# Rstd divided out of the residual around four feed-forwards, their seven products chained through one bank, and own tiles for weight sums

## The chip, the cores and the metric

The kernel runs on one core of a Trainium2 chip. The metric is the device time of one execution in microseconds. TensorE multiplies, VectorE and ScalarE read the results out of the PSUM banks and do the elementwise work, GpSimd takes some of it, and SyncE issues the loads of the weights.

## The reference

The inputs are 512 tokens of width 1024 in float32. A first block (attention of two kinds, then a feed-forward with a short convolution) is followed by a second block of two layers. Each layer of the second block has two feed-forwards with half weight and a mixer between them:

```python
def swiglu(x, w_gate, w_up, w_down):
    return (jax.nn.silu(x @ w_gate) * (x @ w_up)) @ w_down
...
    for l in range(DEPTH_2):
        h = x + 0.5 * swiglu(rms_norm_2(x, ffn1_norm[l]), ffn1_gate[l], ffn1_up[l], ffn1_down[l])
        u = rms_norm_2(h, mix_norm[l])
        ...
        h = h + jnp.concatenate([y_da, y_sc, y_lru], axis=-1) @ w_out[l]
        x = h + 0.5 * swiglu(rms_norm_2(h, ffn2_norm[l]), ffn2_gate[l], ffn2_up[l], ffn2_down[l])
    return rms_norm_2(x, final_norm)
```

The gate and up matrices are 1024 x 2816, the down matrix 2816 x 1024. The change concerns these four feed-forwards.

## The kernel before

The running output `xT` lies in SBUF with features on partitions: eight tiles `xT[:, k, :]` of 128 features by 512 tokens. Every float32 operand of a product is split into a rounded part (`hi`, a ScalarE copy, L155) and a remainder (`lo`, a VectorE subtraction, L159), and a product is three passes: hi x hi, hi x lo, lo x hi. Three pairs of buffers hold split weights (`halves`), five hold weights as loaded (`weights2`).

The hidden 2816 features are worked off in eleven pairs of 128-feature tiles (`pair(t)` in `swiglu_pair`). For each pair, gate and up together are a 2 x 2 block product with half the tokens by half the features, done in seven products in place of eight (`seven`, L225). A product is 24 matmuls of 256 columns (L239 to L241). Weights of the products are sums of blocks: `seven_weights` makes them on VectorE (L209) in a buffer `sums` from the pool `big`, which has two buffers. Pairs alternate between two sets of three banks, (mm, mm, mm) and (sc, sc, o); inside a pair the seven products go to the banks a, d, b, a, b, d, b, and those that return to a bank are accumulated on what stands there:

```python
        for i, (bank, (xh, xl)) in enumerate(zip((a, d, b, a, b, d, b), x)):
```

The seven activations come from `Seven.add` and `Seven.put` (L355 to L388). As each output tile k becomes final, it is multiplied by the gain into `xg`, two tiles of the pool `big`; its squares are added to `acc`. After k = 3 the activations 1 and 5 are split; after k = 7 the other five (L380 to L387).

The normalisation is not applied to the activations: R, the reciprocal root of the mean square, is a row per token that multiplies the results. `Norm.step` first sums `acc` over partitions on TensorE (L261), then VectorE adds eps (L252) and GpSimd takes the power (L247); at its second call TensorE spreads the result over all partitions (L269) and ScalarE copies it to `norm.R` (L287). In a pair, R multiplies the gate before the silu on VectorE and after it on GpSimd (both L1227, a helper's line), so that the product with the up half carries it once more.

`ffn` (L1202) runs `pair` eleven times. From the fourth pair on, each is followed by half a down group: 48 matmuls of 512 columns into two banks `ptr` (L181 to L183), which take two finished pairs to four of the eight output tiles, and `update` adds -0.5 times the bank to `xT` (L1374). The last six tiles come in one group at the end; there `update` also calls `nxt.add`. In the last feed-forward this group is done with tokens on partitions (`final`).

The second block's tables (bias, lambda factors, polynomial for a softplus, block-diagonal weights) are made where the block begins, between the first block's last down product and the first pair (L1303 to L1362).

Each engine runs its instructions in the order of its own queue. That order is made by a scheduler when the kernel is built: it follows the order of the program and takes an instruction early where it expects its inputs and buffers to be there. A tile pool's buffer is given out again after the last read of what was in it.

## Time and profile before

| | us |
|---|---|
| median of three runs | 2653.69 (2651.96 to 2656.13) |
| the profiled execution | 2657.64 |
| its span, first to last instruction | 2655.8 |

The profile shows for each engine when it was busy and what ended its idle time; L12 is line 12 of the kernel. Busy time of TensorE includes matmuls that are stretched or overlap. PEclk is the granted share of TensorE's full clock. "Waits" puts a wait for several things down to the last of them. Below, the head of a feed-forward is the time from its first product to its first down product.

### The profile page before, as it was taken

To read this page: it belongs to the slowest core of one execution; us is meant where nothing else is said; L and a number is where in the kernel's file an instruction comes from. 1 tells how busy PE (TensorE), PEld (TensorE's weight loads), DVE (VectorE), ACT (ScalarE), POOL (GpSimd) and SP (SyncE) were. 2 spreads that over 40 slices of the span, in tenths; PEclk is the share of its full clock that TensorE was granted. 3 is DMA by queue.
4 is the path that set the end of the run, shared out by engine and by line. 5 is a ranking of instruction groups with operands and counts; after the bars stand their busy time and mean duration, and the time that the engine had idled before them with its cause. 6 is when DMAs were issued, how large, how long until landed. Compare 5 with 4: busy or idle time off the path is not lost.

```text
span 2655.8 us, 38263 instructions
## 1 busy us (share of the span) xinstructions
PE 2525.5 (95%) x15256; PEld 2189.1 (82%) x15256; DVE 1963.0 (74%) x2887; ACT 1189.1 (45%) x1758; POOL 435.9 (16%) x334
## 2 busy tenths in 40 slices
PE   5999989999979999999989999899999999899998
PEld 4886668888868999887789999799988877789998
DVE  8788786555589787666688887798886566798774
ACT  4357644333344434356344433544344455444433
POOL 3256220000011111023111111011110222011110
PEclk9999999999989999999989999899999999899999
DMA  8332253333233332421223333233333312233331
GB/s 255 115 107 64 72 159 96 93 91 95 87 113 96 98 108 93 139 72 56 80 72 104 106 101 96 73 103 104 104 96 104 119 56 72 63 103 98 104 108 68
DMA packets 318774, 261.62 MB, mean 99 GB/s; under 512 B 10203, under 2 KB 310619, under 8 KB 318596
## 3 DMA queue, kind: packets, MB, share of 16 engines
q1 hardware_dynamic: 313184, 250.98, 30.8%
q10 hardware_dynamic: 5412, 8.20, 0.9%
q8 instruction: 120, 1.97, 0.3%
q14 instruction: 58, 0.48, 0.1%
HBM read 257.03 MB, written 4.74 MB: 99 GB/s over the span
## 4 chain that ended last, share of the span: by engine, by line
PE 47%; DVE 13%; DMA 4%; issue 3%; ACT 2%; POOL 1%; DVEq 0%; POOLq 0%; ACTq 0%; SPq 0%
PE ptr L181 5%; PE ptr L182 4%; PE ptr L183 4%; PE pmm L239 4%; PE pmm L240 4%; PE pmm L241 4%; DVE lo L159 4%; DMA raw<-in_ffn_up 4%; PE pmm L181 3%; PE pmm L183 3%; PE pmm L182 3%; DVE uf L1227 2%; DVE g L1227 2%; PE psc L240 1%; PE psc L239 1%
## 5 line engine op out<-in xcount | busy, mean ns | idle before, releaser
L155 ACT ACTIVATE hi<-raw 128x1024 fp32r<-128x1024 f32 (+3 forms) x434 | 448.5, 1034 | 649.5 <-issue 165.4
L159 DVE TENSOR_TENSOR lo<-raw,hi 128x1024 fp32r<-128x1024 f32 (+2 forms) x402 | 490.0, 1220 | 239.9 <-ACT hi L155 239.4
L239 PE MATMUL pmm<-gh,hi 128*128 128x256 f32 x1344 | 383.1, 285 | 12.9 <-DVE u L1227 9.3
L241 PE MATMUL pmm<-gh,lo 128*128 128x256 f32 x1344 | 380.9, 284 | 2.3 <-DVE lo L159 2.3
L240 PE MATMUL pmm<-gl,hi 128*128 128x256 f32 x1344 | 380.8, 283 | 0.0
L1227 POOL TENSOR_TENSOR g<-g,R 128x512 f32<-128x512 f32 x88 | 167.9, 1908 | 1067.6 <-ACT g L1240 1067.6
L181 PE MATMUL ptr<-uh,hi 128*128 128x512 f32 x832 | 331.0, 398 | 8.8 <-DVE xT L1374 5.0
L183 PE MATMUL ptr<-uh,lo 128*128 128x512 f32 x832 | 329.0, 395 | 0.0
L182 PE MATMUL ptr<-ul,hi 128*128 128x512 f32 x832 | 328.8, 395 | 0.0
L239 PEld LDWEIGHTS pmm<-gh,hi 128*128 128x128 f32 x1344 | 258.8, 193 | 16.3 <-ACT hi L155 14.3
L241 PEld LDWEIGHTS pmm<-gh,lo 128*128 128x128 f32 x1344 | 259.5, 193 | 3.1 <-DVE lo L159 3.0
L240 PEld LDWEIGHTS pmm<-gl,hi 128*128 128x128 f32 x1344 | 256.9, 191 | 0.9
L155 ACT ACTIVATE hi<-sums 128x1024 fp32r<-128x1024 f32 x132 | 139.7, 1059 | 212.6 <-PE ptr L182 119.7
L181 PEld LDWEIGHTS ptr<-uh,hi 128*128 128x128 f32 x832 | 156.1, 188 | 59.0 <-issue 18.6
L183 PEld LDWEIGHTS ptr<-uh,lo 128*128 128x128 f32 x832 | 156.2, 188 | 37.8
L182 PEld LDWEIGHTS ptr<-ul,hi 128*128 128x128 f32 x832 | 156.3, 188 | 34.0
L241 PE MATMUL psc<-gh,lo 128*128 128x256 f32 x640 | 180.0, 281 | 1.0 <-DVE lo L159 1.0
L239 PE MATMUL psc<-gh,hi 128*128 128x256 f32 x640 | 179.3, 280 | 0.0
L240 PE MATMUL psc<-gl,hi 128*128 128x256 f32 x640 | 179.2, 280 | 0.0
L159 DVE TENSOR_TENSOR lo<-sums,hi 128x1024 fp32r<-128x1024 f32 x132 | 160.2, 1214 | 9.1 <-ACT hi L155 8.9
L181 PE MATMUL pmm<-hh,hi 128*128 128x512 f32 x400 | 159.5, 400 | 3.4 <-ACT hh L745 2.3
L183 PE MATMUL pmm<-hh,lo 128*128 128x512 f32 x400 | 158.8, 398 | 2.8 <-DVE lo L159 2.8
(404 smaller groups left out, 5863.7 us busy)
## 6 DMA issues: line engine op xcount, KB each, us to landing
raw<-in_ffn_gate SPq DMA_DIRECT2D x88, 512.0 KB, 3.6
raw<-in_ffn_up SPq DMA_DIRECT2D x88, 512.0 KB, 3.6
raw<-in_ffn_down SPq DMA_DIRECT2D x64, 512.0 KB, 3.4
raw<-in_w_in SPq DMA_DIRECT2D x60, 512.0 KB, 3.9
raw<-in_w_up SPq DMA_DIRECT2D x44, 512.0 KB, 3.8
wa<-in_w_ada SPq DMA_DIRECT2D x80, 256.0 KB, 2.9
raw<-in_ffn_down SPq DMA_DIRECT2D x32, 384.0 KB, 3.4
raw<-in_w_down SPq DMA_DIRECT2D x16, 512.0 KB, 3.3
```

Source lines behind the costliest of these rows:

```text
L155: nc.scalar.activation(out=hi, in_=v, func=AF.Copy)
L159: e.tensor_tensor(out=lo, in0=v, in1=hi.bitcast(F32), op=ALU.subtract)
L181: mm(ps, hi[:, k, c], xh, start=(k == 0), stop=False)
L182: mm(ps, hi[:, k, c], xl, start=False, stop=False)
L183: mm(ps, lo[:, k, c], xh, start=False, stop=(k == kt - 1))
L239: mm(o, hi[:, k, c], xh[:, k, :], start=first, stop=False, skip_group_check=True)
L240: mm(o, hi[:, k, c], xl[:, k, :], start=False, stop=False, skip_group_check=True)
L241: mm(o, lo[:, k, c], xh[:, k, :], start=False, stop=(j == 1 and k == 3), skip_group_check=True)
L1227: tt = lambda e, out, a, b, op: e.tensor_tensor(out=out, in0=a, in1=b, op=op)
```

## The change

- `seven` sends the seven products to the banks b, d, b, a, b, d, b: four of them are now accumulated in b one after the other, and what each partial sum is needed for is copied out (`s`, `s5`, `w`, on ScalarE) or added to a copy (`g1`, `v2`, `g2`) before the next product goes in. The last sum in b is multiplied with the gate straight from the bank.
- R multiplies only the gate before the silu, now on VectorE for both halves; the products with R on GpSimd go. In their place `over_rstd` divides `xT` by R before the first down group is added (`norm.inverse()`: reciprocal, eight small matmuls for the rows, a copy, and one multiplication for each tile), and multiplies it by R again after the last. In the final stage the factors ride in a copy's scale and in the scalar of the update.
- `norm.step()` stands after the third product and `norm.now()` after the fourth, both with high priority for the scheduler.
- Even pairs take the weight sums from a pool of their own of two tiles (`sums`), odd pairs from `big` as before.
- The second block's tables are made in the first block's feed-forward, at its fifth pair, with a tile of `big` as scratch; its pool `u4` has eight buffers in place of nine.
- Pools of the feed-forwards and the mixer are opened with `reuse_waits="tile"`, so that a new tile waits for the old tiles in its place and not for the whole pool.

```diff
-    def seven_weights(self, srcs):
+    def seven_weights(self, srcs, odd):
 
         a11, a21, a22 = (self.load(src, 4, 256) for src in srcs[:3])
         add = lambda o, p, q: self.nc.vector.tensor_tensor(out=o, in0=p, in1=q, op=ALU.add)
-        sums = self.big("sums").rearrange("p (s k c) -> p s k c", s=2, k=4)
-        s1, s2 = sums[:, 0], sums[:, 1]
+
+        if odd:
+            sums = self.big("sums").rearrange("p (s k c) -> p s k c", s=2, k=4)
+            s1, s2 = sums[:, 0], sums[:, 1]
+        else:
+            s1, s2 = (self.quad(self.ap, n, F32).rearrange("p (k c) -> p k c", k=4) for n in ("s1", "s2"))
         yield self.piece(a11)
         add(s1, a21, a22)
         yield self.piece(s1)
...
-        for i, (bank, (xh, xl)) in enumerate(zip((a, d, b, a, b, d, b), x)):
+        ws = self.seven_weights(srcs, odd)
+        for i, (bank, (xh, xl)) in enumerate(zip((b, d, b, a, b, d, b), x)):
             hi, lo = next(ws)
             for j in range(2):
                 o, c = bank[:, j * HALF:j * HALF + HALF], slice(j * P, j * P + P)
                 for k in range(4):
 
-                    first = i < 3 and j == 0 and k == 0
+                    first = i in (0, 1, 3) and j == 0 and k == 0
                     mm(o, hi[:, k, c], xh[:, k, :], start=first, stop=False, skip_group_check=True)
                     mm(o, hi[:, k, c], xl[:, k, :], start=False, stop=False, skip_group_check=True)
...
+    def inverse(self):
+
+        if self.inv is None:
+            net = self.net
+            self.inv = net.up.tile([P, T], F32, tag="inv", name="inv", bufs=1)
+            ic = net.tiny(NB, "ic")
+            net.nc.vector.reciprocal(out=ic, in_=self.rc)
+            net.nc.scalar.activation(out=self.inv, in_=net.rows(ic), func=AF.Copy)
+        return self.inv
 
     def after(self, tiles):
...
 
-    with tc.tile_pool(name="u4", bufs=U_BUFS) as net.up, tc.tile_pool(name="ada2", bufs=2) as adap:
+    bp = net.ctx.enter_context(tc.tile_pool(name="b2", bufs=1))
+    tables = []
+    with tc.tile_pool(name="u4", bufs=U_BUFS - 1, reuse_waits="tile") as net.up, \
+            tc.tile_pool(name="ada2", bufs=2, reuse_waits="tile") as adap:
         mods = ada(range(20, 24), adap)
 
         def pair(t):
+            if t == 8:
+                tables.extend(second_block_tables(net, bp))
             for _ in range(2):
...
 
-    def down(g0, n, chunks, last):
+    def down(i, g0, n, chunks):
         for ci in chunks:
             src = wd[g0 * P:(g0 + n) * P, ci * 256:(ci + 1) * 256]
             for j, ps in net.lin_fm(src, n, 256, us[g0:g0 + n], net.ps_tr):
-                update(2 * ci + j, ps, last)
+                update(2 * ci + j, ps, i)
 
     for g in range(NFF // 2):
         us += pair(2 * g)
         if g >= 3:
             i, hf = divmod(g - 3, 2)
-            down(4 * i, 4, (2 * hf, 2 * hf + 1), False)
+            down(i, 4 * i, 4, (2 * hf, 2 * hf + 1))
     if last_group is None:
-        down(16, 6, range(4), True)
+        down(LAST, 16, 6, range(4))
     else:
         last_group(16, 6, us[16:22])
 
 
+def over_rstd(net, norm, k, ps, i):
+
+
+    v, xk = net.nc.vector, net.xT[:, k, :]
+    if i == 0:
+        v.tensor_tensor(out=xk, in0=xk, in1=norm.inverse(), op=ALU.mult)
+    v.scalar_tensor_tensor(out=xk, in0=ps, scalar=-0.5, in1=xk, op0=ALU.mult, op1=ALU.add)
+    if i == LAST:
+        v.tensor_tensor(out=xk, in0=xk, in1=norm.R, op=ALU.mult)
+
+
 def swiglu_pair(net, x, norm, wg, wu):
 
     nc = net.nc
     tt = lambda e, out, a, b, op: e.tensor_tensor(out=out, in0=a, in1=b, op=op)
-    v, g_ = nc.vector, nc.gpsimd
+    v = nc.vector
     two = lambda t: t.rearrange("p (j t) -> p j t", j=2)
 
     def pair(t):
         c = slice(t * P, t * P + 256)
         srcs = (wg[0:T, c], wu[0:T, c], wu[T:2 * T, c], wg[T:2 * T, c])
         ps = net.seven(srcs, x, (t // 2) % 2)
-        s, s5, u2, u3, g1, g2 = (net.ev(n) for n in ("s1", "s5", "u2", "u3", "g1", "g2"))
+        s, s5, w, v2, g1, g2 = (net.ev(n) for n in ("s1", "s5", "w", "v2", "g1", "g2"))
         uf = net.quad(net.up, "uf", F32).rearrange("p (j t) -> p j t", j=2)
+        copy = lambda out, src: nc.scalar.activation(out=out, in_=src, func=AF.Copy)
 
         def gate(g, i):
             R = norm.R[:, i * HALF:i * HALF + HALF].unsqueeze(1).to_broadcast([P, 2, HALF])
+            tt(v, two(g), two(g), R, ALU.mult)
             nc.scalar.activation(out=g, in_=g, func=AF.Silu)
-            tt(g_, two(g), two(g), R, ALU.mult)
-
-        def scale(out, src, i):
-            R = norm.R[:, i * HALF:i * HALF + HALF].unsqueeze(1).to_broadcast([P, 2, HALF])
-            tt(v, two(out), two(src), R, ALU.mult)
-
-        nc.scalar.activation(out=s, in_=next(ps), func=AF.Copy)
-        nc.scalar.activation(out=s5, in_=next(ps), func=AF.Copy)
-        tt(v, u2, next(ps), s, ALU.add)
-        norm.step()
-        bank = next(ps)
-        norm.now()
-        scale(g1, bank, 0)
+
+        copy(s, next(ps))
+        copy(s5, next(ps))
+        copy(w, next(ps))
+        with net.tc.high_priority():
+            norm.step()
+        tt(v, g1, next(ps), s, ALU.add)
+        with net.tc.high_priority():
+            norm.now()
+        tt(v, v2, next(ps), s5, ALU.add)
         gate(g1, 0)
-        tt(v, u3, next(ps), s, ALU.add)
-        tt(v, u3, u3, s5, ALU.add)
-        tt(v, g2, next(ps), u2, ALU.add)
-        scale(g2, g2, 1)
+        tt(v, g2, next(ps), w, ALU.add)
         gate(g2, 1)
-        tt(v, s, next(ps), s, ALU.add)
-        tt(v, uf[:, :, 0:HALF], two(s), two(g1), ALU.mult)
-        tt(v, uf[:, :, HALF:T], two(u3), two(g2), ALU.mult)
+        tt(v, uf[:, :, 0:HALF], two(next(ps)), two(g1), ALU.mult)
+        tt(v, uf[:, :, HALF:T], two(v2), two(g2), ALU.mult)
         hi, lo = (net.quad(net.up, n).rearrange("p (j t) -> p j t", j=2) for n in ("uh", "ul"))
         nc.scalar.activation(out=hi, in_=uf, func=AF.Copy)
         tt(v, lo, uf, hi.bitcast(F32), ALU.subtract)
...
+def second_block_tables(net, bp):
+
+    nc, a, tc = net.nc, net.a, net.tc
+    tmp = net.big("tmp")
+    flat = bias_tables(net, tmp)
...
-            net.up = up.enter_context(tc.tile_pool(name=f"u4{l}", bufs=U_BUFS))
+            net.ap = up.enter_context(tc.tile_pool(name=f"sums{l}", bufs=2, reuse_waits="tile"))
+            net.up = up.enter_context(tc.tile_pool(name=f"u4{l}", bufs=U_BUFS, reuse_waits="tile"))
...
-                net.sp = c2.enter_context(tc.tile_pool(name=f"singles{l}", bufs=S_BUFS))
-                net.zp = c2.enter_context(tc.tile_pool(name=f"z{l}", bufs=Z_BUFS))
+                net.sp = c2.enter_context(tc.tile_pool(name=f"singles{l}", bufs=S_BUFS, reuse_waits="tile"))
+                net.zp = c2.enter_context(tc.tile_pool(name=f"z{l}", bufs=Z_BUFS, reuse_waits="tile"))
...
+        update = lambda k, ps, i: over_rstd(net, norm, k, ps, i)
...
-                    nc.scalar.activation(out=xk[tb][:, hf, :], in_=ps, func=AF.Copy)
+                    nc.scalar.activation(out=xk[tb][:, hf, :], in_=ps, func=AF.Identity, scale=norm.rc[:, tb:tb + 1])
+
+            rh = net.tiny(NB, "rh")
+            nc.vector.tensor_scalar(out=rh, in0=norm.rc, scalar1=-0.5, scalar2=None, op0=ALU.mult)
...
                     xc = xk[tb][:, ci // 2, (ci % 2) * 256:(ci % 2) * 256 + 256]
-                    nc.vector.scalar_tensor_tensor(out=xc, in0=ps[:, :256], scalar=-0.5, in1=xc,
```

## Rows read from the trace of the kernel before

**Rows 1.** The page, busy time of each engine.

```profile
PE 2525.5 (95%) x15256; PEld 2189.1 (82%) x15256; DVE 1963.0 (74%) x2887; ACT 1189.1 (45%) x1758; POOL 435.9 (16%) x334
```

**Rows 2.** Windows, four heads: us, busy (count) PE, PEld, DVE, ACT, POOL, PEclk, DMA.

```profile
739.40:847.40 108.00, 88.01 (x693) 85.17 (x693) 95.49 (x130) 50.67 (x59) 16.30 (x9) 0.91 0.35 113
1332.80:1430.20 97.40, 84.32 (x689) 82.85 (x688) 88.00 (x92) 49.13 (x56) 15.03 (x8) 0.93 0.30 91
1695.10:1795.20 100.10, 86.95 (x690) 85.45 (x689) 91.26 (x92) 47.92 (x56) 13.75 (x8) 0.90 0.29 89
2278.40:2376.20 97.80, 84.12 (x690) 82.25 (x689) 88.04 (x92) 49.13 (x56) 15.13 (x8) 0.93 0.29 91
```

**Rows 3.** Windows: one later group, columns as above.

```profile
1474.10:1505.30 31.20, 31.05 (x217) 28.48 (x216) 25.42 (x28) 12.45 (x15) 3.95 (x2) 1.00 0.27 85
```

**Rows 4.** Timeline of TensorE, end of the mixer and second head.

```profile
1288.15 1.16 PE L269 MATMUL ptr<-ident,rp 128*128 128x128 f32 x8 [1.04 <-POOL rp L247]
...
1336.44 1.02 PE L261 MATMUL ptr<-ones,acc 128*128 128x1 f32 x8 [0.77 <-DVE acc L321]
1345.28 2.08 PE L269 MATMUL ptr<-ident,rp 128*128 128x128 f32 x8 [7.82 <-POOL rp L247]
...
1348.99 0.58 PE L239 MATMUL pmm<-gh,hi 128*128 128x256 f32 x1 [1.21 <-ACT hi L155]
```

**Rows 5.** Timeline of VectorE at the second head.

```profile
1337.35 4.62 DVE L359 TENSOR_TENSOR gl<-xg,gh 128x1024 fp32r<-128x1024 f32 x4
1341.89 1.22 DVE L386 SCALAR_TENSOR_TENSOR xg<-xg 128x1024 f32<-128x1024 f32 x1
1343.03 0.15 DVE L252 TENSOR_SCALAR var<-ptr 128x4 f32<-128x4 f32 x1
1343.14 1.23 DVE L209 TENSOR_TENSOR sums<-raw 128x1024 f32<-128x1024 f32 x1
```

**Rows 6.** Timeline of TensorE at the first head.

```profile
742.30 1.24 PE L1282 MATMUL ptr<-onehot,rel 33*8 33x512 f32 x4
749.36 1.87 PE L261 MATMUL ptr<-ones,acc 128*128 128x1 f32 x8 [5.83 <-DVE tb L1283]
757.37 2.07 PE L269 MATMUL ptr<-ident,rp 128*128 128x128 f32 x8 [6.13 <-POOL rp L247]
```

**Rows 7.** Waits, whole span: total, times, longest.

```profile
DVE xT L1394 <- PE pmm L183: 29.6, 12, 2.9
...
PE pmm L239 <- DVE u L1227: 9.3, 7, 1.9
...
PE ptr L181 <- DVE xT L1374: 5.0, 10, 1.3
...
PE po L239 <- DVE u L1227: 4.7, 5, 1.9
```

**Rows 8.** Windows: the third pair of the second head.

```profile
1388.10:1410.30 22.20, 20.21 (x171) 19.83 (x170) 20.25 (x22) 10.39 (x12) 4.22 (x2) 1.00 0.30 96
```

**Rows 9.** Windows: behind a wait of 1.88 us.

```profile
1771.90:1775.30 3.40, 3.40 (x18) 3.40 (x17) 3.40 (x5) 0.00 (x0) 0.00 (x0) 0.50 0.48 159
```

**Rows 10.** Groups by line, whole span.

```profile
L1227 POOL TENSOR_TENSOR g<-g,R 128x512 f32<-128x512 f32 x88 | 167.9, 1908 | 1067.6 <-ACT g L1240 1067.6
...
L1227 DVE TENSOR_TENSOR uf<-s,g 128x512 f32<-128x512 f32 x44 | 64.1, 1456 | 0.0
...
L1227 DVE TENSOR_TENSOR uf<-u,g 128x512 f32<-128x512 f32 x44 | 30.0, 683 | 13.6 <-POOL g L1227 13.6
```

**Rows 11.** Waits, and two groups by line, of ScalarE, whole span.

```profile
ACT hi L155 <- PE pmm L240: 187.1, 106, 6.0
...
L155 ACT ACTIVATE hi<-raw 128x1024 fp32r<-128x1024 f32 (+3 forms) x434 | 448.5, 1034 | 649.5 <-issue 165.4 <-PE pmm L182 159.2 <-PE pmm L240 139.5
...
L1247 ACT ACTIVATE s<-pmm 128x512 f32<-128x512 f32 x24 | 13.9, 581 | 2.6 <-DMA wl<-in_lru_wx 2.6
```

**Rows 12.** Windows: first block's feed-forward, about one group.

```profile
505.00:539.00 34.00, 34.00 (x147) 27.28 (x146) 18.73 (x24) 11.79 (x15) 0.00 (x0) 1.00 0.31 93
```

More of the change, by code (lines that the diff above doesn't have):

```diff
@@ L809, in first_block @@
     net.dump("x1", xT)
-    return nxt
+    return nxt, tables
 def first_body(net):
@@ L1323, in second_block @@
-        nc.vector.tensor_tensor(out=nlam, in0=ls[:, 2:4], in1=ls[:, 0:2], op=ALU.subtract)
-        gsub = bp.tile([P, 2], F32, name="gsub")
-        linit = [0.8 - 0.6 * math.exp(-0.3 * l) for l in range(2)]
-        for l in range(2):
-            nc.vector.tensor_scalar(out=nlam[:, l:l + 1], in0=nlam[:, l:l + 1], scalar1=-linit[l], scalar2=None,
-                                    op0=ALU.add)
-            nc.vector.tensor_scalar(out=gsub[:, l:l + 1], in0=col(net, "subln_gain_2", l), scalar1=1.0 - linit[l],
-                                    scalar2=None, op0=ALU.mult)
@@ L1342, in second_block @@
-        v.tensor_tensor(out=z2, in0=z_, in1=z_, op=ALU.mult)
-        v.memset(pl, 1.0 / 19)
-        for d in range(17, 0, -2):
-            v.tensor_tensor(out=pl, in0=pl, in1=z2, op=ALU.mult)
-            v.tensor_scalar(out=pl, in0=pl, scalar1=1.0 / d, scalar2=None, op0=ALU.add)
-        v.tensor_tensor(out=pl, in0=pl, in1=z_, op=ALU.mult)
-        v.tensor_scalar(out=pl, in0=pl, scalar1=16.0, scalar2=None, op0=ALU.mult)
-        v.tensor_scalar(out=sp8, in0=lam, scalar1=-8.0, scalar2=0.0, op0=ALU.mult, op1=ALU.max)
@@ L1350, in second_block @@
-        v.tensor_tensor(out=sp8, in0=sp8, in1=pl, op=ALU.add)
-        nsp8 = t4("nsp8")
-        v.tensor_scalar(out=nsp8, in0=sp8, scalar1=-1.0, scalar2=None, op0=ALU.mult)
-        tmp.close()
-        wl = bp.tile([P, 2, 4, P], F32, name="wl")
-        nc.gpsimd.memset(wl, 0.0)
-        for g, name in enumerate(("lru_wa_2", "lru_wx_2")):
-            src = a[name].rearrange("(n s) i j -> s i n j", s=2)
-            for s in range(2):
-                nc.scalar.dma_start(out=wl[64 * s:64 * s + 64, g, :, 64 * s:64 * s + 64], in_=src[s])
@@ L1371, in second_block, with update @@
             nxt = Gained(net, col(net, "mix_norm_2", 8 * l, 8))
-            def update(k, ps, last):
-                nc.vector.scalar_tensor_tensor(out=xT[:, k, :], in0=ps, scalar=-0.5, in1=xT[:, k, :],
-                                               op0=ALU.mult, op1=ALU.add)
-                if last:
+            def update(k, ps, i):
+                over_rstd(net, norm, k, ps, i)
+                if i == LAST:
                     nxt.add(xT[:, k, :])
@@ L1405, in second_block @@
                 else:
-                    final(net, pair, a["ffn2_down_2"][l])
+                    final(net, norm, pair, a["ffn2_down_2"][l])
 class HeadDiff:
@@ L1592, in mixer, with final @@
     return mix
-def final(net, pair, wd):
+def final(net, norm, pair, wd):
     nc, a = net.nc, net.a
@@ L1601, in final @@
         ssq = fp.tile([P, NB, 4], F32, name="ssq")
-        def update(k, ps, last):
-            nc.vector.scalar_tensor_tensor(out=xT[:, k, :], in0=ps, scalar=-0.5, in1=xT[:, k, :],
-                                           op0=ALU.mult, op1=ALU.add)
+        update = lambda k, ps, i: over_rstd(net, norm, k, ps, i)
         def last_group(g0, n, us):
```

97 lines of the change are left out of this document (60 added, 37 removed).

## The prediction

> **What bounds the kernel now.** I read the page's shares first: TensorE is busy for 95% of the span [rows 1], but that share counts matmuls that are stretched or overlap, so I went on to its busy time by stretches. Between the first product of a feed-forward and its first down product lie four pairs of products and nothing else for TensorE. In those four stretches, one for each feed-forward of the second block, it is busy 84 to 88 us of 97 to 108, and the granted clock is 0.90 to 0.93 [rows 2]. Later in the same feed-forward a group of one pair and half a down group takes 31.2 us, TensorE has work for 31.05 of them, and the clock is 1.00 [rows 3]. That group is 168 matmuls of 256 columns and 48 of 512: 264 units of 256 columns, 0.118 us each, so a pair costs 168 x 0.118 = 19.85 us, and four 79.4. The stretches take 108.0, 97.4, 100.1 and 97.8: 28.6, 18.0, 20.7 and 18.4 more than that, 85.7 us in all. The later groups are full; what can be won lies at the heads of the feed-forwards.
>
> Then the order of time at the second head, engine by engine. TensorE does the first product, sums the squares (L261), and stands 7.82 us before the rows of the reciprocal (L269), which queue ahead of the second product; they then run at half clock (2.08 us; a later one at full clock took 1.16), and 1.21 us more are lost on a weight copy [rows 4]. VectorE shows why: between the squares and the variance (L252) stand L383, four remainders of the split activations and L386, 1.22 us each alone; an instruction of 0.15 us comes out at 1343.03, 5.6 us after its input. The first weight sum (L209) comes right behind, at 1343.14: it writes a "big" buffer, and both are held by the gained activations until L386 has read them [rows 5]. So two things release the second product at the same time: the normalisation, and the sums' buffers. The first head is longer, since the second block's tables lie in it: L1282 takes both small banks, L261 waits 5.83 us until they are copied out, L269 another 6.13 [rows 6]. From the second pair on, TensorE waits for VectorE's reads of the reused bank (L239 behind u, 14.0 us in all, 1.9 at most) [rows 7]: VectorE is busy 20.25 us in the third pair, more than TensorE's 19.85 [rows 8].
>
> **The change part by part.** *Own tiles for sums.* The first pair no longer needs a big buffer. Its first sum, copy and remainder can run while the last products of the stage before still occupy TensorE. The second product can follow the first; it needs the activations made from the first four tiles, which are long there.
>
> *Normalisation moved and given priority.* Squares and rows are issued after the third and fourth product, ahead of other ready work. Variance no longer stands behind the splits, and no bank's read needs R before the last. The two groups of small products still cost 1.02 and 1.16 at full clock, 2.2 [rows 4].
>
> *What is late next.* VectorE still has all the splits. From 1334.5 I lay out its work at the 1.15 us that four in 4.62 take [rows 5]: acc 0.6, L380 1.15, the first remainder until about 1339. TensorE, through two products at 1338.4, waits 0.8 for it. The other splits come earlier in program order than the fourth product's weight remainder: four remainders and two more operations put that at about 1345, where the third product ends at about 1342: 3.1 us. The fifth needs a sum, a copy and a remainder behind it: 1.3. Half-clock time behind such waits: after a wait of 1.9 us, 18 matmuls took 3.40 us at clock 0.50, the 1.2 GHz level [rows 9], where 18 x 0.118 make 2.1; that is 1.3 for one wait, and I take 1.7 for these together. For bubbles in the next three pairs I leave 1.0 (before, the third pair alone took 22.2, 2.35 over [rows 8]). Head: 2.2 + 0.8 + 3.1 + 1.3 + 1.7 + 1.0 = 10.1 us over the floor, against 18.0 and 18.4: a gain of 7.9 and 8.3. In the third, the last tile also gets a multiplication by R, 0.7 us (as the multiplication at 0.68) [rows 10]: 20.7 - 10.8 = 9.9. In the first, with the tables gone, 28.6 - 10.1 = 18.5. Sum 44.6. Bounds: 10.1 could be 3.2 (the small products and 1.0), or as long as now less only the pairs' bubbles.
>
> *Evacuation.* Of VectorE's operations in a pair (ten without weights), eight stay; ScalarE gets one copy of 0.58 [rows 11], and both GpSimd products go. Two operations saved are 1.2 us at their spacing, and the product s x g, 1.46 us on average where the same shape without GpSimd beside it takes 0.68, loses another 0.8 [rows 10]: 20.2 becomes about 18.2, under TensorE's 19.85. This is the 1.0 above; in the full groups VectorE is not the bound (25.4 of 31.2 [rows 3]), so there it pays nothing. A rule bears on the size. The Trainium skill's page "SBUF — State Buffer" (section "Who interferes with whom") states that VectorE and GpSimd share a port pair under an exclusive lock, the loser blocked for the whole instruction. By that, two products of 1.9 us could take up to 3.8 us a pair from VectorE, and the rival in which all waits go would be likelier; the row's 0.8 says that most of it doesn't meet, and I keep 0.8.
>
> *Chaining.* Bank b is rewritten at products 3, 5 and 7, before at 5 and 7. Two of its three reads are now ScalarE copies with one product, 24 x 0.118 = 2.83 us, as cover. A copy of 0.58 behind two weight copies of 1.03 is 2.64 [rows 11]: just inside. I take 0; bounds 0 and 1.9 us, the longest such wait now [rows 7], per read.
>
> *Rstd divided out.* In each of four feed-forwards: reciprocal, rows (1.16 us of TensorE at full clock, always added: 4.6 in all), a ScalarE copy of 0.58 [rows 11], eight multiplications on VectorE. The latter are 5.5 us beside two groups of 31.2 with 5.8 us idle each [rows 3]: hidden. But the first down bank can't be freed until rows, copy, multiplication and update (1.16 + 0.58 + 0.68 + 0.68 = 3.1) are through, and there are two such banks; if they are issued ahead, nothing waits. Now the down products wait for updates 5.0 us at ten places [rows 7]. I take 1.0 for each, 4.0; bounds 0 and 3.1. The multiplication by R at the end is on the way to the mixer twice, but its first product uses the last tile last: 0, at most 1.4. In the final stage the factors ride in operations that exist: 0.
>
> *Tables moved.* Some 40 small VectorE operations, four matmuls (1.24 us [rows 6]), table loads, a GpSimd memset and twelve DMA issues of ScalarE now fall into the first block's feed-forward at its fifth pair. There TensorE is busy 34.0 of 34.0, VectorE 18.7, ScalarE 11.8 [rows 12]: those two hide theirs, SP's queue isn't passed, and GpSimd is idle. ScalarE's queue will stand while the small scratch table goes out and before it is read back, with conv evacuations behind it; three banks, each a product of 24 x 2 x 0.118 = 5.7 us, cover that. The matmuls cost 1.24, and I add 1.0 for the two small banks they share with down: 2.2; bounds 1.2 and 8 (the first head's 5.83 again). One buffer fewer for u: pairs before the down group wait for it already with nine, so 0; at most a down half-group's order. Finer waits on pool reuse: the mixer's start shows no wait worth naming, 0.
>
> Sum: -44.6 + 4.6 + 4.0 + 2.2 = -33.8 us. The profiled execution took 2657.64 (span 2655.8), so it would take 2623.8; the three runs' median is 3.95 lower, which gives 2620.
>
> **Rivals.** *All waits go* (17%): VectorE runs ahead far enough that each head keeps 3.2 us. 85.7 - 4 x 3.2 = 72.9 gained, 6.8 paid (rows, tables, a stall or two less): 66, 2588. For it: VectorE idles up to 2.9 us at each of the last tiles of the mixer's output [rows 7]. Against: its 10 us of splits come in one piece behind the last tile.
>
> *The head stays VectorE's* (19%): splits in front of the fourth product's weights, or the rows still queued too early on TensorE, keep 15 us or so of the 18. Then the tables' 10.3 (28.6 - 18.3) and 2 us in each of four stretches are won, 18.3, and 10.8 paid: -7.5, 2646. This is also the case in which priority doesn't change the order.
>
> *The chain makes every pair wait* (8%, the other side): ScalarE's queue is in order, and weight copies stand in it until TensorE frees a buffer, 187.1 us over 106 waits, 6.0 at most [rows 11]. If a third weight copy stands before a bank copy, that is 0.58 + 3 x 1.03 - 2.83 = 0.84 late: 88 copies x 0.84 = 74, less 33.8: 40 slower, 2694. It decides from 33.8 / 88 = 0.38 us per copy on. Against it: ScalarE is busy 12.45 of 31.2 [rows 3], and a weight copy and a bank copy are released by the same product. The Trainium skill, "TensorE: Matmul & The Clock Gate", section on PSUM-queue depth-cycling, speaks for it: cycling through banks makes micro-idles, and the clock then oscillates. By that rule each such wait would bring half-clock time too; rows 9 show this once at a wait of 1.9, and no full group shows it.
>
> Something unforeseen in the changed queue orders of the other stages, to the slower side: 4%. My forecast has the remaining 52%.
>
> **How the numbers follow.** 2620 is the likeliest case. Its own range, with stalls of the down banks and heads between their bounds, is 2603 to 2638. The range 2588 to 2650 takes in the third case and half of the second; below lies about 6%, above 13%. What a measurement here can tell from no change is 0.2%, 5.3 us. Faster: 52 + 17 + 14 of the 19 = 83%; same 6%; slower 11%.
>
> **What would show it.** Right: the four stretches at about 89.5 us with PEclk over 0.95; L269 without a wait over 2 us; the first head no longer than the others; GpSimd's L1227 gone; no PE wait on copies in full groups. Wrong: L239 waiting for s or w throughout (the chain), L181 or the new rows waiting 2 us or more at the first down (division), or VectorE without idle time for 20 us while TensorE stands (splits).

## The result, and the profile after

The changed kernel takes 2593.28 us (median of four, 2590.92 to 2599.84), the kernel before on the same chip 2654.91 (2651.96 to 2656.48): a ratio of 0.9773, 95% interval 0.9752 to 0.9794, 61.6 us faster. The forecast was 33.8 us faster. The profiled execution took 2595.03, with a span of 2593.2. In the changed code the products are L245 to L247 (before L239 to L241), the down products L183 to L185, squares and rows L267 and L275 (before L261 and L269), weight sums L211, weight remainders L161, splits L375.

The page's busy times: GpSimd has lost 167 of its 436 us [rows 1], and TensorE, with 12.8 us less of busy time, has a larger share.

```profile
PE 2512.7 (97%) x15288; PEld 2188.8 (84%) x15288; DVE 1903.2 (73%) x2860; ACT 1214.8 (47%) x1804; POOL 269.2 (10%) x246
```

Windows of the changed kernel: the four heads, and one later group (columns as in rows 2).

```profile
744.40:835.90 91.50, 83.84 (x690) 82.48 (x689) 82.06 (x87) 49.77 (x60) 1.92 (x1) 0.94 0.31 99
1318.20:1401.20 83.00, 80.43 (x689) 79.28 (x688) 76.43 (x82) 50.31 (x59) 1.92 (x1) 1.00 0.32 102
1664.10:1753.30 89.20, 84.64 (x689) 83.33 (x688) 80.15 (x86) 49.83 (x59) 1.85 (x1) 0.96 0.32 101
2234.30:2318.00 83.70, 81.06 (x689) 80.09 (x688) 76.55 (x83) 50.35 (x60) 1.92 (x1) 1.00 0.33 101
...
1444.50:1475.50 31.00, 31.00 (x217) 28.80 (x216) 24.20 (x26) 13.23 (x15) 0.00 (x0) 1.00 0.29 94
```

Against [rows 2] the heads lose 16.5, 14.4, 10.9 and 14.1: 55.9 us. The stretches from a head's end to the next head, or to the end of the span, go from 485.4, 264.9, 483.2 and 279.6 to 482.3, 262.9, 481.0 and 275.2: 11.7 us less, although each has the eight new rows. The time up to the first head grows from 739.4 to 744.4. The sum is 62.6, the difference of the spans.

TensorE's timeline at the first and the second head:

```profile
748.30 1.05 PE L267 MATMUL ptr<-ones,acc 128*128 128x1 f32 x8
751.62 2.08 PE L275 MATMUL ptr<-ident,rp 128*128 128x128 f32 x8 [2.26 <-POOL rp L253]
757.72 0.58 PE L247 MATMUL pmm<-gh,lo 128*128 128x256 f32 x1 [4.03 <-DVE lo L161]
...
1322.40 1.02 PE L267 MATMUL ptr<-ones,acc 128*128 128x1 f32 x8 [0.32 <-DVE acc L337]
1325.68 1.16 PE L275 MATMUL ptr<-ident,rp 128*128 128x128 f32 x8 [0.85 <-POOL rp L253]
```

At the second head the 7.82 us of [rows 4] have become 0.85, and the rows run in 1.16. The first head still waits 4.03 for a weight remainder. VectorE's timeline there shows why:

```profile
744.63 0.75 DVE L824 SCALAR_TENSOR_TENSOR xT<-ptr,mod,xT 128x512 f32<-128x512 f32 x1 [1.44 <-PE ptr L185]
745.30 1.22 DVE L211 TENSOR_TENSOR s<-raw 128x1024 f32<-128x1024 f32 x1
...
749.47 3.49 DVE L375 TENSOR_TENSOR gl<-xg,gh 128x1024 fp32r<-128x1024 f32 x3
752.88 1.22 DVE L402 SCALAR_TENSOR_TENSOR xg<-xg 128x1024 f32<-128x1024 f32 x1
755.30 1.22 DVE L375 TENSOR_TENSOR gl<-xg,gh 128x1024 fp32r<-128x1024 f32 x1 [1.21 <-ACT gh L374]
756.45 1.22 DVE L161 TENSOR_TENSOR lo<-s,hi 128x1024 fp32r<-128x1024 f32 x1
```

The first weight sum comes at 745.30, behind the last update; its remainder, which the second product needs, stands behind four splits. At the second head that sum is made at 1296.18, 22 us ahead of the head.

The two steps of the normalisation stood behind the third and the fourth product in the kernel before, too; the change gives them priority and doesn't move them. With priority their matmuls run early: at the second head the squares come after 33 matmuls of the products and the rows after 44, so both lie inside the second product.

Groups by line of the changed kernel: the product that took 1456 ns beside GpSimd [rows 10] takes 682 from the bank.

```profile
L1259 DVE TENSOR_TENSOR uf<-v,g 128x512 f32<-128x512 f32 x44 | 29.9, 681 | 0.0
...
L1259 DVE TENSOR_TENSOR uf<-pmm,g 128x512 f32<-128x512 f32 x24 | 16.4, 682 | 0.0
```

### The profile page after: what moved, and what is told of

Its sections match the earlier page's. It is cut to its first block, busy times and chain, and to the rows that moved or that the text cites. A ratio compares the mean times of both kernels' runs of the same rounds, so it can differ in the third digit from the quotient of the medians.

```text
span 2593.2 us, 38138 instructions
## 1 busy us (share of the span) xinstructions
PE 2512.7 (97%) x15288; PEld 2188.8 (84%) x15288; DVE 1903.2 (73%) x2860; ACT 1214.8 (47%) x1804; POOL 269.2 (10%) x246
## 3 DMA queue, kind: packets, MB, share of 16 engines
q1 hardware_dynamic: 313184, 250.98, 31.4%
## 4 chain that ended last, share of the span: by engine, by line
PE 49%; DVE 2%; ACT 1%; POOL 1%; issue 0%; DMA 0%; DVEq 0%; POOLq 0%; ACTq 0%; SPq 0%
PE ptr L183 4%; PE ptr L184 4%; PE ptr L185 4%; PE pmm L245 4%; PE pmm L247 4%; PE pmm L246 4%; PE pmm L183 3%; PE pmm L185 3%; PE pmm L184 3%; PE po L245 2%; PE po L246 2%; PE po L247 2%; PE psc L247 2%; PE psc L246 2%; PE psc L245 2%; PE pmm L203 1%
## 5 line engine op out<-in xcount | busy, mean ns | idle before, releaser
L161 DVE TENSOR_TENSOR lo<-raw,hi 128x1024 fp32r<-128x1024 f32 (+2 forms) x402 | 482.4, 1201 | 219.4 <-ACT hi L157 213.6
L247 PE MATMUL pmm<-gh,lo 128*128 128x256 f32 x1344 | 378.8, 282 | 5.7 <-DVE lo L161 5.6
L245 PE MATMUL pmm<-gh,hi 128*128 128x256 f32 x1344 | 379.9, 283 | 3.1 <-ACT hi L157 2.5
L183 PE MATMUL ptr<-uh,hi 128*128 128x512 f32 x832 | 330.2, 397 | 0.2 <-ACT hi L157 0.2
L185 PE MATMUL ptr<-uh,lo 128*128 128x512 f32 x832 | 329.0, 395 | 0.0
L253 POOL TENSOR_TENSOR rp<-var,neghalf 128x4 f32<-128x4 f32 (+2 forms) x46 | 56.8, 1236 | 1989.8 <-DVE var L258 1989.6
L245 PEld LDWEIGHTS pmm<-gh,hi 128*128 128x128 f32 x1344 | 258.4, 192 | 5.5 <-ACT hi L157 3.1
L247 PEld LDWEIGHTS pmm<-gh,lo 128*128 128x128 f32 x1344 | 254.0, 189 | 6.6 <-DVE lo L161 6.6
L183 PEld LDWEIGHTS ptr<-uh,hi 128*128 128x128 f32 x832 | 156.7, 188 | 37.4 <-ACT inv L308 0.8
L185 PEld LDWEIGHTS ptr<-uh,lo 128*128 128x128 f32 x832 | 156.3, 188 | 37.8
L245 PE MATMUL po<-gh,hi 128*128 128x256 f32 x640 | 179.6, 281 | 1.7 <-ACT hi L157 1.7
L246 PE MATMUL po<-gl,hi 128*128 128x256 f32 x640 | 179.2, 280 | 0.0
L247 PE MATMUL po<-gh,lo 128*128 128x256 f32 x640 | 179.1, 280 | 0.0
L183 PE MATMUL pmm<-hh,hi 128*128 128x512 f32 x400 | 160.6, 403 | 6.2 <-ACT hh L761 3.3
L185 PE MATMUL pmm<-hh,lo 128*128 128x512 f32 x400 | 160.5, 402 | 3.8 <-DVE lo L161 3.8
L184 PE MATMUL pmm<-hl,hi 128*128 128x512 f32 x400 | 160.1, 401 | 0.0
L157 ACT ACTIVATE hi<-s 128x1024 fp32r<-128x1024 f32 x72 | 76.6, 1064 | 171.1 <-PE ptr L184 114.5
```

The costliest lines, as they stand in the source:

```text
L157: nc.scalar.activation(out=hi, in_=v, func=AF.Copy)
L161: e.tensor_tensor(out=lo, in0=v, in1=hi.bitcast(F32), op=ALU.subtract)
L183: mm(ps, hi[:, k, c], xh, start=(k == 0), stop=False)
L184: mm(ps, hi[:, k, c], xl, start=False, stop=False)
L185: mm(ps, lo[:, k, c], xh, start=False, stop=(k == kt - 1))
L245: mm(o, hi[:, k, c], xh[:, k, :], start=first, stop=False, skip_group_check=True)
```

## The experiments

Two theories stood against each other: that two releases (own sums, early normalisation) carry the heads, as the prediction had it, and that the relief of VectorE, by fewer operations or by the end of its collisions with GpSimd, carries the gain. A collision is an operation of VectorE that takes longer because one of GpSimd's runs at the same time. Heads are in us, the ratio is to the kernel before on the same chip.

| kernel | 1st | 2nd | 3rd | 4th | ratio (95%) |
|---|---|---|---|---|---|
| before | 108.0 | 97.4 | 100.1 | 97.8 | 1 |
| changed | 91.5 | 83.0 | 89.2 | 83.7 | 0.9773 (0.9752 to 0.9794) |
| changed, second chip | 92.0 | 84.2 | 89.7 | 84.6 | 0.9755 (0.9734 to 0.9776) |
| before + own sums | 108.6 | 86.7 | 92.6 | 86.7 | 0.9890 (0.9871 to 0.9910) |
| before + own sums + priority | 111.3 | 91.2 | 88.8 | 92.7 | 0.9916 (0.9900 to 0.9933) |
| before, no GpSimd products | 101.2 | 92.6 | 92.9 | 94.3 | 0.9838 (0.9822 to 0.9854) |
| changed, sums in big | 93.9 | 94.8 | 95.0 | 95.0 | 0.9861 (0.9836 to 0.9885) |
| changed, activations scaled | 96.4 | 89.0 | 90.7 | 89.0 | 0.9804 (0.9789 to 0.9818) |
| changed, old banks | 91.9 | 85.5 | 91.4 | 84.6 | 0.9780 (0.9753 to 0.9808) |
| changed, tables at the block's start | 105.5 | 83.3 | 90.3 | 84.7 | 0.9781 (0.9765 to 0.9797) |
| changed, no division | 92.2 | 83.9 | 83.7 | 83.3 | 0.9706 (0.9692 to 0.9721) |
| changed, no priority | 91.1 | 82.9 | 87.9 | 82.7 | 0.9726 (0.9705 to 0.9746) |
| the same, sums behind u4 | 83.1 | 81.9 | 86.3 | 81.9 | 0.9697 (0.9682 to 0.9711) |
| the same, R in the last hidden tiles | 83.6 | 83.1 | 83.8 | 81.9 | 0.9701 (0.9686 to 0.9716) |

**Own sums alone, on the kernel before.** The edit is the diff's first hunk with the pool that it needs.

> The kernel before with one part of the change: even pairs take the weight sums from their own two tiles; nothing else. Theory of the two releases (own sums and the earlier normalisation carry the heads): half of it is here, so the second product's weights come early, while the rows of R still stand behind VectorE's splits; heads about 4 us shorter each, 2635 to 2645 against 2654.9 for the kernel before. Rival (relief of VectorE and the end of its collisions with GpSimd carry the gain): the heads stay at 97 to 100, 2650 to 2657.

29 us faster by the ratio (the profiled execution was the slowest of its four, and its span is only 17.2 shorter). Heads two to four lose 10.7, 7.5 and 11.1; the first, with the tables in it, nothing. TensorE's timeline at the second head has squares and rows without a wait, although they have no priority here and VectorE's splits are the same; the squares now come behind the second product:

```profile
1342.97 0.95 PE L264 MATMUL ptr<-ones,acc 128*128 128x1 f32 x8
...
1346.84 0.60 PE L272 MATMUL ptr<-ident,rp 128*128 128x128 f32 x4
```

But the full groups get longer: from the start of one pair to the next 31.6 us in the median, where it was 31.4. A group's window, and the wait of down products for updates, which had been 5.0 us at ten places [rows 7]:

```profile
1467.90:1499.70 31.80, 31.30 (x218) 28.69 (x217) 25.66 (x28) 12.65 (x15) 3.94 (x2) 1.00 0.29 84
```

```profile
PE ptr L181 <- DVE xT L1378: 10.6, 21, 1.4
```

So own sums release the heads, the rows of R with them, and later updates in the full groups take part of it back.

**Own sums and priority, on the kernel before.**

```diff
-        norm.step()
+        with net.tc.high_priority():
+            norm.step()
         bank = next(ps)
-        norm.now()
+        with net.tc.high_priority():
+            norm.now()
```

> The kernel before with own sums and with priority for the two steps of the normalisation; banks, scaled activations on GpSimd and tables as before. Theory of the two releases: this is all that the heads need; second and fourth about 86, third about 91, first about 98 (the tables still lie in it), 2616 +- 8. Rival (relief of VectorE): with VectorE's work and the GpSimd products as before the heads stay at 92 or more, 2640 or more.

It missed: slower than own sums alone in its median (2640.99 against 2632.90, though the ranges of the four times overlap), with the second and fourth heads 4.5 and 6.0 longer and the third 3.8 shorter. The two releases together don't bring the heads to 86; the first theory falls as the whole explanation.

**The changed kernel with sums from the big buffers.**

```diff
-        if odd:
+        if True:
             sums = self.big("sums").rearrange("p (s k c) -> p s k c", s=2, k=4)
...
```

> The changed kernel with all weight sums from the two big buffers again. Theory that own sums and relief of VectorE add up: the second product waits for the gained activations again, and what own sums gave to the kernel before, 29 us in three heads, is lost here in four: 25 to 38 us slower. Rival: with the normalisation early and GpSimd quiet, VectorE reads the gained activations out sooner, and only 2 to 3 us per head come back: 10 us.

28.6 us slower than the changed kernel on its chip. TensorE's timeline at the second head of this run has the wait that own sums take away; at each head it is 6.31:

```profile
1336.96 0.58 PE L245 MATMUL pmm<-gh,hi 128*128 128x256 f32 x1 [6.31 <-ACT hi L157]
```

The price of 29 us holds from both sides.

**The kernel before without the GpSimd products.**

```diff
             nc.scalar.activation(out=g, in_=g, func=AF.Silu)
-            tt(g_, two(g), two(g), R, ALU.mult)
```

> The kernel before without the second multiplication of the gate by R: both GpSimd products of each pair are left out, nothing takes their place (the product with the up half then carries R once less). Theory of the collision: VectorE's product s x g goes from 1.46 to 0.68 us, the update behind it comes in time and the full groups go from 31.3 to 31.0 (some 32 half groups, 9 us), and the heads lose 2 to 4 us each: 18 to 26 us faster, about 0.991. Rival: VectorE's count of operations makes the groups long; they stay at 31.3 and the time within 5 us.

More than either theory gave: a ratio of 0.9838, 43 us. The heads lose 22.3 together, and the four stretches behind them 3.5, 3.1, 3.7 and 4.8, 15.1 in all; the time up to the first head, where these products don't occur, is 4.7 shorter too, which the edit doesn't explain. A full group takes 31.00, and VectorE is busy for 46.7 us less over the whole span than in [rows 1], with the same 2887 instructions:

```profile
1452.70:1483.70 31.00, 31.00 (x217) 28.80 (x216) 24.82 (x28) 12.74 (x14) 0.00 (x0) 1.00 0.30 86
```

```profile
PE 2509.8 (96%) x15256; PEld 2186.2 (84%) x15256; DVE 1916.3 (73%) x2887; ACT 1192.9 (46%) x1758; POOL 268.5 (10%) x246
```

VectorE has the same number of operations in that group as in [rows 3], so in the full groups it is the collision and not the count. At the heads the run doesn't separate the collision from VectorE's waits for GpSimd's result (13.6 us at 13 places over the span, [rows 10]), which end with the products too. How a full group lost time shows in the timeline of the kernel before, all engines, in a full group:

```profile
1495.41 2.14 POOL L1227 TENSOR_TENSOR g<-g,R 128x512 f32<-128x512 f32 x1 [6.80 <-ACT g L1240]
...
1496.32 1.78 DVE L1227 TENSOR_TENSOR uf<-s,g 128x512 f32<-128x512 f32 x1
...
1498.03 0.68 DVE L1227 TENSOR_TENSOR uf<-u,g 128x512 f32<-128x512 f32 x1
...
1498.63 0.68 DVE L1374 SCALAR_TENSOR_TENSOR xT<-ptr,xT 128x512 f32<-128x512 f32 x1
...
1498.91 0.40 PE L183 MATMUL ptr<-uh,lo 128*128 128x512 f32 x1
...
1499.46 0.47 PE L181 MATMUL ptr<-uh,hi 128*128 128x512 f32 x1
```

The product that takes 0.68 alone takes 1.78 beside GpSimd's; the update behind it is 1.1 late, and the third output of the half group, which needs that bank, starts at 1499.46 in place of 0.23 behind 1498.91. Of this gap of 0.32 the modelled end of the matmul before covers 0.17, which counts as busy, and the remaining 0.15 is all of the group's idle time in [rows 3]. The starts of the matmuls between 1480 and 1640 show such a gap in each of the five groups there, 0.19 to 0.45 us, always at that place; the same stretch of this run and of the changed kernel has none. From the start of one pair to the next a full group took 31.2 to 31.7, with few exceptions, and now takes 31.0. The Trainium skill, "SBUF — State Buffer", section "Who interferes with whom", states an exclusive lock between the two. The rows agree with it: VectorE's product ends 0.55 us after GpSimd's, less than its own 0.68, so that it stood still for nearly all of the overlap; of the 44 products s x g, 37 ran beside one of GpSimd's and took 1.60 in the mean, the other seven 0.68.

**The changed kernel with activations scaled as before.**

```diff
             nc.scalar.activation(out=g, in_=g, func=AF.Silu)
+            tt(nc.gpsimd, two(g), two(g), R, ALU.mult)
...
-    if i == 0:
-        v.tensor_tensor(out=xk, in0=xk, in1=norm.inverse(), op=ALU.mult)
...
-    if i == LAST:
-        v.tensor_tensor(out=xk, in0=xk, in1=norm.R, op=ALU.mult)
...
```

The final stage's two factors go as well.

> The changed kernel with the activations scaled as before: R multiplies both gates again after the silu on GpSimd, and nothing is divided out of the running output. Theory of the two releases: heads as in the changed kernel within 1 us, and four times 1.05 us of rows saved, 2589. Rival (relief): VectorE's product from the bank collides with GpSimd again, each of some 32 half down groups waits 0.3 us for a late update, and the pairs of the heads stretch by about 2 us each: 2593 + 10 + 8 - 4 = 2607.

0.9804: the second theory's place, but not its mechanism. The full groups stay at 31.0, although GpSimd's second product still runs at the same time as VectorE's product from the bank. Of the 44 of these, 32 ran beside it and took 0.68 as the others did:

```profile
1473.64 1.49 POOL L1255 TENSOR_TENSOR g<-g,R 128x512 f32<-128x512 f32 x1 [5.27 <-ACT g L1270]
...
1473.89 0.68 DVE L1255 TENSOR_TENSOR uf<-po,g 128x512 f32<-128x512 f32 x1
```

The slow product of the kernel before read `s` and `g`, both in SBUF; this one reads one of its two inputs from a PSUM bank. So with the chain, which leaves the last sum in the bank, the full groups lose nothing to GpSimd's products. All of the loss is at the heads, 4.9, 6.0, 1.5 and 5.3. The timeline of all engines in the second head, fourth pair:

```profile
1392.82 2.08 POOL L1255 TENSOR_TENSOR g<-g,R 128x512 f32<-128x512 f32 x1 [5.36 <-ACT g L1270]
...
1394.93 0.69 DVE L1255 TENSOR_TENSOR uf<-v,g 128x512 f32<-128x512 f32 x1 [1.19 <-POOL g L1255]
...
1395.65 1.06 ACT L1288 ACTIVATE uh<-uf 128x1024 fp32r<-128x1024 f32 x1 [1.67 <-DVE uf L1255]
...
1396.62 0.58 ACT L1265 ACTIVATE s<-po 128x512 f32<-128x512 f32 x1
...
1397.25 0.38 PE L245 MATMUL po<-gh,hi 128*128 128x256 f32 x1 [1.46 <-ACT s L1265]
```

VectorE waits for GpSimd, ScalarE's copy for the split waits for VectorE, and the bank copy `s` stands behind it in ScalarE's queue, so that the next product in the chained bank is 1.46 late. At the heads the chain bears no GpSimd in its loop.

This run leaves the division out too, which costs time of its own (below). Set against the changed kernel without the division, from which it differs by GpSimd's products and the final stage's factors, its heads are 22.0 longer together and the stretches behind them the same. At the heads these products cost as much here as in the kernel before (22.3).

**The changed kernel with the old banks**, two operations more on VectorE and a copy fewer on ScalarE in each pair.

```diff
-        for i, (bank, (xh, xl)) in enumerate(zip((b, d, b, a, b, d, b), x)):
+        for i, (bank, (xh, xl)) in enumerate(zip((a, d, b, a, b, d, b), x)):
...
-        tt(v, uf[:, :, 0:HALF], two(next(ps)), two(g1), ALU.mult)
+        tt(v, s, next(ps), s, ALU.add)
+        tt(v, uf[:, :, 0:HALF], two(s), two(g1), ALU.mult)
...
```

> The changed kernel with the seven products sent to the banks a, d, b, a, b, d, b as before and the partial sums read as before: one more addition on VectorE and the last sum read out before the product with the gate (two operations more on VectorE, one copy fewer on ScalarE in each pair); R still only on VectorE and divided out of the running output. If VectorE's count of operations made the full groups 0.3 us longer before, they are 31.3 again, and heads grow by 1 to 2 us each: 10 + 6, about 1.006 of the changed kernel. Rival: the collision with GpSimd had made them longer; then they stay at 31.0 and the time within 4 us.

The groups stay at 31.0, as the rival has it, but the time grows by more than its 4 us. The medians differ by 6.2 us, and the four times of each kernel on the same chip don't overlap (2600.89 to 2608.65 against 2595.47 to 2600.24), though the intervals of the ratios do. In the two profiles the heads together are 2.9 longer and the stretches behind them 3.9. With GpSimd's products gone the chain is worth some 6 us, a part of it at the heads.

**The changed kernel as it is**, beside the two undone parts above and the one below; its row stands in the table.

> The changed kernel as it is, on the chip of the three that follow, so that their heads can be set against its own: 0.977 of the kernel before, heads near 91, 83, 89 and 84.

**The changed kernel without priority** for the two normalisation steps.

```diff
-        with net.tc.high_priority():
-            norm.step()
+        norm.step()
...
-        with net.tc.high_priority():
-            norm.now()
+        norm.now()
```

> The changed kernel without the priority of the two normalisation steps; they stay at their places. Theory of the prediction: squares and rows fall behind the splits again and R comes late: heads about 5 us longer, 20 us in all. Rival, after the run of own sums with and without priority (1.003 slower with it): the first operation that needs R stands behind the fourth product anyway, so that the order without priority is as good or better: 0 to 8 us faster.

The rival was right: 2588.27 to 2591.13 against 2595.47 to 2600.24 on the same chip, each head 0.9 to 1.9 shorter (the intervals of the ratios overlap). The spans of the two profiles differ by 8.8 us; 5.9 of it lies in the heads, and 3.8 ahead of the first, which the edit doesn't touch. The first head remains at 91.1, with a wait of 6.89 us for the remainder that the second product needs:

```profile
750.27 0.58 PE L247 MATMUL pmm<-gh,lo 128*128 128x256 f32 x1 [6.89 <-DVE lo L161]
```

**The same with the sums' pool opened behind u4**, so that the tiles lie elsewhere in SBUF.

```diff
-            net.ap = up.enter_context(tc.tile_pool(name=f"sums{l}", bufs=2, reuse_waits="tile"))
             net.up = up.enter_context(tc.tile_pool(name=f"u4{l}", bufs=U_BUFS, reuse_waits="tile"))
+            net.ap = up.enter_context(tc.tile_pool(name=f"sums{l}", bufs=2, reuse_waits="tile"))
...
```

> The changed kernel without the priority, and with the pool of the sums opened behind the pool u4 instead of ahead of it, so that at the first head the sums don't lie where the stage before still reads its hidden tiles. Theory: the first head is long because the first weight sum must wait for the last down product (745.30 against 744.2), so that its remainder falls behind the splits; freed from that, the first head goes from 91.2 to 83 to 86 and the others stay: 5 to 8 us faster than without the priority alone, about 0.970 of the kernel before. Rival: the splits of the last output tile hold the head up whatever the sums do; 91 and no difference.

The first head goes to 83.1. VectorE's timeline has the sum and its remainder early:

```profile
728.48 1.22 DVE L211 TENSOR_TENSOR s<-raw 128x1024 f32<-128x1024 f32 x1
...
740.37 1.22 DVE L161 TENSOR_TENSOR lo<-s,hi 128x1024 fp32r<-128x1024 f32 x1
```

So where the pool of the sums lies was the rest of the first head. That in the changed kernel the sums lie on the first block's hidden tiles is argued from the order in which the pools are opened; the trace shows no addresses. At 2584.61 this version beats both kernels. The gain over the run without priority is smaller than the first head's 8.0: the spans differ by 4.6, since the time ahead of that head is 5.0 longer in this profile, and the intervals of the ratios overlap slightly.

**The changed kernel without the division.**

```diff
-    if i == 0:
-        v.tensor_tensor(out=xk, in0=xk, in1=norm.inverse(), op=ALU.mult)
...
-    if i == LAST:
-        v.tensor_tensor(out=xk, in0=xk, in1=norm.R, op=ALU.mult)
```

> The changed kernel with the division of the running output by R and the multiplication at the end left out, with the reciprocal, the rows and the copy that make the divisor (the final stage's factors stay). Prediction's terms: 4.6 for the rows and 4.0 for waits at the first down banks come back, 8 to 9 us faster than the changed kernel. Rival: only the rows cost anything, four times 1.05: 4 us faster, and the third head 1 us shorter.

The division costs more than both said, but elsewhere: 13 to 18 us by the ratios, 10.3 by the spans of the profiles. Three of the stretches behind the heads get 0.8, 1.1 and 1.1 shorter and one 0.7 longer, the time ahead of the first head 3.6 shorter, and the third head 5.5. No wait at the first down bank was there to take away. At the third head it is the multiplication by R behind the last down group that loads VectorE; in the changed kernel two of its eight operations stand in VectorE's queue around the start of that head (1664.1), ahead of most of its splits:

```profile
1662.65 0.68 DVE L1253 TENSOR_TENSOR xT<-xT,R 128x512 f32<-128x512 f32 x1
...
1665.59 0.68 DVE L1253 TENSOR_TENSOR xT<-xT,R 128x512 f32<-128x512 f32 x1
```

The run with R in the last hidden tiles, below, moves them. What the division costs outside the third head isn't assigned.

**R in the last hidden tiles**, to move that multiplication.

```diff
-    if i == LAST:
+    if i == LAST - 1 and early:
         v.tensor_tensor(out=xk, in0=xk, in1=norm.R, op=ALU.mult)
...
+            twice = t >= 16 and not last
...
+            if twice:
+                tt(v, two(g), two(g), R, ALU.mult)
```

> The run before (no priority, sums behind u4), and the multiplication of the running output by R taken off the last update: in the three feed-forwards that use it, the last six hidden tiles carry R a second time (two products more on VectorE in three pairs), and the running output is multiplied by R behind the fourth down group, two pairs before the end. Theory: the multiplication in the last group delays VectorE's work for the third head; that head goes from 86.3 to 82 to 84, the mixers' starts win up to 1 us each; 0.968 of the kernel before. Rival: the third head is longer for another reason (the splits, as everywhere); 86 again, 0.970, or slower by up to 3 us for the products added.

The third head goes from 86.3 to 83.8, as the theory had it; the total doesn't change by what can be measured (0.9701 against 0.9697). The third head thus has the level that it has without the division, 83.7.

**The tables at the block's start again**, in the changed kernel.

```diff
-            if t == 8:
-                tables.extend(second_block_tables(net, bp))
...
```

The scratch is a tile of its own again.

> The changed kernel with the second block's tables made where the block begins, as before. Theory of the prediction: the tables lengthen the first head by some 10 us (91.5 to about 101) and give back 2 to 5 us in the first block: 2598 to 2601. Rival: with the sums' own tiles the first products no longer need what the tables hold up, so that the tables hide at the head as well and only the 2 to 5 us come back: 2588 to 2591.

The first head is 105.5, 14 longer, and TensorE waits 8.00 us for the tables' bank:

```profile
751.14 1.87 PE L267 MATMUL ptr<-ones,acc 128*128 128x1 f32 x8 [8.00 <-DVE tmp L1307]
```

The time up to this head is 739.0, 5.4 shorter than with the tables there. By the profiles the move is worth some 9 us; by the times it isn't settled, since the interval overlaps those of the changed kernel.

## Why the prediction was right or wrong

The direction and the chief place were right; the size was not: 62.6 us of span in place of 33.8. The 2593.28 us lie below the 2603 to 2638 that the prediction gave its likeliest case, and near the 2588 of the rival in which all waits go. That this rival's total comes so close is luck: it wanted 72.9 from the heads, which gave 55.9, and nothing from the stretches behind them, which gave 11.7. By terms:

- *Heads, -44.6.* Measured -55.9. What is left over four pairs (79.4) is 12.1, 3.6, 9.8 and 4.3, where 10.1, 10.1, 10.8 and 10.1 stood. In the second and fourth the terms 3.1 and 1.3 for waits behind splits, and 1.7 for half clock, didn't come: the scheduler put weight remainders between the splits, and the clock was 1.00. Those two heads went the way of the rival in which all waits go.
- *First head no longer than the others*: wrong, 91.5; the squares' rows waited 2.26, over the 2 set. The tables' wait went as forecast, and a cause that the prediction didn't see took its place: where the pool of the sums lies, worth 8 us of that head. That the first sum can be made while the stage before still occupies TensorE held for the second head, with 22 us to spare, and not for the first.
- *Own sums* as a release: right, and 29 us from both sides. *Normalisation moved and given priority*, the second release: wrong. Nothing was moved, and at the second head squares and rows ran inside the second product, not behind the third and fourth. Own sums alone already took away the 7.82 us before the rows [rows 4], so that there was one release and not two; the order without priority was better. (The rows of 1.16 us at full clock [rows 4], a later one in the prediction, are an earlier one; the price holds.)
- *Evacuation: "so there it pays nothing"* in the full groups. This is the step that failed, and the largest miss: for the stretches behind the heads the sum had 8.6 us more (rows and stalls of the division), and they lost 11.7, which is 20.3 of the 28.8 us that the sum is short. TensorE's 31.05 of 31.2 us [rows 3] was read as full; a stall of 0.2 to 0.5 a group was in it, behind VectorE's collision, and the full group is 31.0. The unit of 0.118 us and the floor of 79.4 hold that stall too; 31.0 would give 0.117 and 78.9. Taking the GpSimd products out of the kernel before shortens the four stretches by 15.1; the change shortens them by 11.7 and has four times 1.05 us of rows to pay, 15.9. The collision was costed at 0.8 us in a pair of [rows 10]; VectorE's busy time fell by 46.7 over 44 pairs, 1.06 in a pair, so that most of the 3.8 set as its bound didn't meet, as was said. But the cost was set against the wrong cover: not VectorE's idle time in the group, but the update behind the product in VectorE's queue, whose bank TensorE needs next.
- *Rstd, 4.6 and 4.0.* The rows take 1.05 each, about what was said; the stall at the down banks didn't exist: at the second feed-forward's first down products TensorE ran nine matmuls of the next pair in between. The third head, where 0.7 was set for the multiplication at the end, loses 5.5 by the division. All in all the division cost 10 to 18 us.
- *Chaining, 0*: right for the waits. No full group has a wait on bank copies, and every group takes the same 31.0 with the chain and without it. The Trainium skill's micro-idles ("TensorE: Matmul & The Clock Gate", PSUM-queue depth-cycling) show in no full group here, at a clock of 1.00. The chain gained some 6 us that the prediction didn't have, and at the heads it needs the short loop without GpSimd. That a sum read straight from its bank isn't slowed beside GpSimd was in no term.
- *Tables, 2.2*: measured 5.0 between the two profiles, with 1.81 for a wait on a weight copy at 488.75 and half clock from 491.1 to 494.5; how much of the rest is the tables' is open (below).

The parts as they were tried, own sums 29, GpSimd's products 43, the chain 6 and the tables some 9, less about 15 for the division and 8 for the priority, come to 64 us, where 61.6 were measured. They were taken from different kernels, so that this agreement is an estimate and no proof. Reuse waits and the smaller `u4` were not tried apart.

## What to carry to other kernels

A busy share near one is no proof of a full engine: compare the starts of equal matmuls with their usual spacing (here 0.23 us for 512 columns), before calling a stage's cover free. When a slow operation is on an in-order queue, cost what stands behind it, not its own length. Where two engines slow each other, see which operands they read: here a product with one input in a PSUM bank ran beside GpSimd unslowed. When a new pool is to release a buffer, look at whose memory it lies on; and when one part of a change is said to help the order, run the change without it.

## What the runs showed of the hardware that was not expected

The time up to the first head varies by more than the edits explain: 744.4 and 742.3 us for the changed kernel in two profiles, 738.5 to 744.9 over the versions with the tables there, 734.8 to 742.0 over those without. Differences of up to some 7 us in that stretch can't be put down to a part from single profiles.

VectorE's 128x512 product beside GpSimd's took 1.60 us in the mean with both inputs in SBUF (37 products of the kernel before) and 0.68 with one of them in a PSUM bank (32 products of the changed kernel with activations scaled as before), the same as alone.
